# Delta rule recurrence with the decayed state written back into a held PSUM bank, and row scaling in 128-column blocks

## The chip, the cores and the metric

One core of a Trainium2 chip runs the whole kernel. The metric is the device time of one execution in microseconds (us); the median of three runs of the kernel before is 1159.26 us (1158.74 to 1159.27).

## The reference

One transformer-like layer over 1024 tokens of width 1024, in float32. Group A of its mixer is a gated delta rule with 4 heads of 128, evaluated in chunks of 64 tokens; the change lies there. Everything else (modulated RMS norms, the short convolution of group B, the products with `w_out`, a SwiGLU with 2816 hidden channels) is matrix products around it.

```python
def step(state, inp):
    qd, wi, ui, ai, kd, gl = inp
    v_new = ui - jnp.einsum('bhcd,bhde->bhce', wi, state)
    out = jnp.einsum('bhcd,bhde->bhce', qd, state) + jnp.einsum('bhcm,bhme->bhce', ai, v_new)
    state = state * jnp.exp(gl)[..., None, None] + jnp.einsum('bhcd,bhce->bhde', kd, v_new)
    return state, out
...
h = rms_norm(x, norm1_w[l]) * (1.0 + scale1) + shift1
x = x + gate1 * hybrid_mixer(h, ...)
h = rms_norm(x, norm2_w[l]) * (1.0 + scale2) + shift2
x = x + gate2 * swiglu(h, w_gate[l], w_up[l], w_down[l])
return rms_norm(x, norm_f_w)
```

The state of a head is 128 x 128. It is multiplied by the chunk's decay, and the product of the chunk's decayed keys and new values is added to it.

## The kernel before

**Stages.** The tokens are handled in two halves of 512 (`hf` 0 and 1). The first stage, up to about 472 us, is written as tasks (`fill`, `gdn`, `merge`, `output`, `mod_rows`, `gate5` and others). While the program is built, a planner (`Sim`) issues their instructions one by one: it keeps a table of costs, computes for each task when its next operation could start, and takes the earliest; among tasks that could start on that engine at the same time the lower number in `PR` wins. So it decides the order of every engine's instructions, and this order is then fixed. What follows from 472 us on (line 89 for TensorE) is written out by hand in a fixed order, and so is not replanned.

**What TensorE runs in between.** `fill` has the lowest priority and feeds TensorE whenever no other task can: first the products of the normed input with `w_in` (tile `acc`, 128x512 with fp32r operands, three for each 128x128 block), then, when these are used up, the products with `w_out` for tokens 0 to 511 (tile `o`, 8 tiles of 24 products). They take three PSUM banks (0 to 2); all other tasks share five (`chb`).

**The recurrence** (`gdn`) runs once per half, eight chunks in a row (`t` 0 to 3, `cc` 0 and 1), for four heads at once. One step: four products `A` (`WQ` with the state `S`, both read in fp32), VectorE subtracts (`A<-u,A`), ScalarE or VectorE copies the part for the output (`qs`), four products `K` (`kt` with the new values) into a fresh bank, and VectorE updates each head's state by one SCALAR_TENSOR_TENSOR `S<-S,egl,K`. After every second chunk four products `O` follow. Before it, `merge` scales `kt` by row factors into `L`, and later `kt` in place; after it, `output` scales `u` by a row factor, transposes it on TensorE (tile `y`), multiplies it by `zt` and, in the second half, splits it into `at` and `kt` for the products with `w_out`. Each of these three scalings is one VectorE TENSOR_TENSOR over 128x512 with a broadcast factor.

**What hangs on the end of the second recurrence.** When its last `output` is done (`("gdn", 1)`), `mod_rows` builds two rows by ones-products on TensorE (tile `row`), `gate5` loads 16 pieces of `w_ada` of 256 KB through SyncE's queue and accumulates them on VectorE (`A<-Tt,c_act,A` and `aacc<-raw,c_act,aacc`), splits the sums into tiles `Tt`; then SyncE loads `x` for tokens 512 to 1023 (512 KB a tile) and stores the four finished `x` tiles of tokens 0 to 511 to `x_scr` (512 KB each), after which VectorE scales these tiles in place (`x<-x,st,u`). The first buffers of those loads are ones that the `row` products and their splits have read, so the loads wait for them.

**The hand-written part** starts with 24 products `o` (`w_out_tile(4, 1)`), then four `row` products that read `gate5`'s tiles `Tt` (`g5_rows`), 24 more `o` products, and 16 transposes `tr` of the four scaled `x` tiles (`first_half`).

Of the kernel before, what the change touches and what calls it, by code (L numbers as in the profile page):

```python
# [17 lines left out]
P = 128  # L18
# [33 lines left out]
def kernel(  # L52
# [53 lines left out]
    def nm(s):  # L106
        n_id[0] += 1
        return f"{s}_{n_id[0]}"
# [193 lines left out]
    class Sim:  # L302
# [261 lines left out]
    def bank(res, name):  # L564
        return res.tile(psp, [P, HT], F32, name)
# [7 lines left out]
    free = sim.free  # L573

    def ecopy(dst, src):
        sim.either([("act", "copy", nc.scalar.copy, (dst, src), {}), ("dve", "tensor_copy", nc.vector.tensor_copy, (dst, src), {})])
# [6 lines left out]
        ecopy(hi, src)  # L583
        DVE.tensor_tensor(lo, src, hi.bitcast(F32), ALU.subtract)

    def mm(out_, lhsT, rhs, start=True, stop=True):
        PE.matmul(out_, lhsT, rhs, start=start, stop=stop)

    def tr(out_, in_):
        PE.transpose(out_, in_, ident)  # L590
# [583 lines left out]
    def merge(hf, h, T, XA, DD):  # L1174
        st, t_ = sc_[hf], T[h]
        u = us[hf]
        L = t_["L"]
        sim.wait(lambda: ("a", hf, h) in done)
        pP = bank(chb, "P")
        for g in range(2):  # L1180
            mm(v3(pP[:, 32 * g:32 * g + P], 4), L[:, 2 * g + 1, :], bc1(DD[:, 1, 2 * h + g, :], 4))
        ecopy(DD[:, 0, 2 * h:2 * h + 2, :], v3(pP[:, 0:64], 2))
        free(pP)
        Tt = gt("Tt")
        DVE.transpose(flat(Tt), flat(xbd[0][:, 4 * h:4 * h + 4, :]))
        pQ = bank(chb, "Q")
        for g in range(2):
            mm(v3(pQ[:, 32 * g:32 * g + P], 4), XA[:, 2 * h + g, :], bc1(DD[:, 0, 2 * h + g, :], 4))
        for p in range(2):
            for c in range(2):  # L1190
                q = 64 * c + 32 - 32 * p
                ecopy(Tt[64 * c:64 * c + 32, p:4:2, 64 * c + 32:64 * c + 64], v3(pQ[q:q + 32, 0:64], 2))
        free(pQ)
        done.add(("q", hf, h))
        DVE.tensor_tensor(t_["L"], t_["kt"], bc2(t_["bk"], P), ALU.mult)
        free(t_["bk"])
        sim.wait(lambda: ("vt", hf, h) in done)
        pu = bank(chb, "u")
        for t in range(4):
            mm(pu[:, tsl(t)], Tt[:, t, :], u[:, h, t, :])  # L1200
        ecopy(flat(u[:, h]), pu)
        free(pu)
        pw = bank(chb, "w")
        for t in range(4):
            mm(pw[:, tsl(t)], t_["L"][:, t, :], Tt[:, t, :])
        free(t_["L"])
        free(Tt)
        ecopy(t_["WQ"].rearrange("p t (c n) -> p t c n", c=4)[:, :, 0:4:3, :],
                 pw.rearrange("p (t c n) -> p t c n", t=4, c=2))
        free(pw)  # L1210
        DVE.tensor_tensor(t_["kt"], t_["kt"], bc2(st["kd"][:, :, h], P), ALU.mult)
        done.add(("uw", hf, h))

    def gdn(hf):
# [53 lines left out]
        VV = gt("A", (P, 2, 4, P))  # L1268
        V, V1 = VV[:, 0], VV[:, 1]
        POOL.memset(VV, 0.0)  # L1270
        for t in range(4):
            qs = gt("qs")
            if t:
                POOL.memset(V[64:128], 0.0)
            for cc in range(2):
                r0 = 64 * cc
                rv, ro = slice(r0, r0 + 64), slice(64 - r0, 128 - r0)
                W = V1 if cc else V
                first, last = hf == t == cc == 0, hf == cc == 1 and t == 3
                if first:  # L1280
                    ecopy(V[rv], u[rv, :, t, :])
                    POOL.memset(qs[ro], 0.0)
                else:
                    pA = bank(chb, "A")
                    for h in heads:
                        mm(pA[:, tsl(h)], T[h]["WQ"][:, t, cc * P:(cc + 1) * P], S[h])
                    DVE.tensor_tensor(W[rv], u[rv, :, t, :], v3(pA, 4)[rv], ALU.subtract)
                    if cc:
                        ecopy(V[rv], V1[rv])
                    ecopy(qs[ro], v3(pA, 4)[ro])  # L1290
                    free(pA)
                if not last:
                    pK = bank(chb, "K")
                    for h in heads:
                        mm(pK[:, tsl(h)], T[h]["kt"][:, t, :], W[:, h, :])
                    for h in heads:
                        if first:
                            S[h] = gp.tile([P, P], F32, name=nm("S"), tag=f"S{h}", bufs=1)
                            ecopy(S[h], pK[:, tsl(h)])
                        else:  # L1300
                            DVE.scalar_tensor_tensor(S[h], S[h], T[h]["egl"][:, t, cc:cc + 1], pK[:, tsl(h)], ALU.mult, ALU.add)
                    free(pK)
            pO = bank(chb, "O")
            for h in heads:
                mm(pO[:, tsl(h)], T[h]["at"][:, t, :], V[:, h, :])
            DVE.tensor_tensor(u[:, :, t, :], v3(pO, 4), qs, ALU.add)
            free(pO)
            free(qs)
        free(VV)
        for h in heads:  # L1310
            for n in ("at", "WQ", "egl", "kt"):
                free(T[h][n])
# [14 lines left out]
    def output(hf, h, T):  # L1327
        u = us[hf]
        o, nq = u[:, h], T[h]["nq"]
        so, junk, rn = gt("so", (P, 4)), gt("jk", (P, P), BF16), gt("ro", (P, 4))  # L1330
        for t in range(4):
            ACT.activation(junk, o[:, t, :], AF.Square, accum_out=so[:, t:t + 1])
        free(junk)
        DVE.scalar_tensor_tensor(so, so, 1.0 / 128.0, nq, ALU.mult, ALU.add)
        free(nq)
        rsqrt_pow(rn, so, 4)
        DVE.tensor_tensor(o, o, bc2(rn, P), ALU.mult)
        free(so)
# [1057 lines left out]
```

## Time and profile before

| | |
|---|---|
| median of three runs | 1159.26 us |
| span of the profiled execution, first to last instruction | 1158.3 us |
| what lies around the span, against the median | 0.96 us |
| granted TensorE clock, mean | 0.998 |
| first recurrence | about 216 to 258 us |
| second recurrence | about 385 to 429 us |
| planned stage ends, hand-written part begins | 471.7 us |

The profiled execution's own time is not listed beside its span; the difference of 0.96 us is taken as what lies around it. In the profile PE is TensorE's matmul, PEld its weight load, DVE VectorE, ACT ScalarE, POOL GpSimd, SP SyncE and SPq its DMA queue. A row of the chain or the timeline gives start and length in us. An fp32 product appears as two records, so a group of four heads is `x8`. Matmuls are pipelined and overlap in the records, so TensorE's busy share is near 100% wherever they follow each other; how fast it goes is read from the length of a run of equal products.

### The profile page before, as it was taken

The page shows a single profiled execution, that of the slowest core. Times are in us where ns is not written, and L with a number is a line of the kernel's source. Part 1 is how long each engine was busy: PE and PEld are TensorE (multiplying, and loading weights), DVE is VectorE, ACT ScalarE, POOL GpSimd, SP SyncE. Part 2 cuts the span into 40 slices and gives each one's busy share as a digit, 9 for nine tenths or more (in the row PEclk, how much of TensorE's full clock was granted, in tenths as well). Part 3 has the DMA queues.
Part 4 walks back from the last instruction along what each step waited for, and adds up shares of the span by engine and source line. Part 5 has one row for each costly group of instructions (what it writes and reads, how often), then busy time and mean ns, then how long its engine had stood idle before and what let it go on. Part 6 is the DMA issues. An engine that isn't in the chain of part 4 may idle for free.

```text
span 1158.3 us, 16873 instructions
## 1 busy us (share of the span) xinstructions
PE 1148.2 (99%) x5682; PEld 967.1 (83%) x5682; DVE 961.4 (83%) x1820; ACT 565.6 (49%) x1244; POOL 62.3 (5%) x100
## 2 busy tenths in 40 slices
PE   8999999999999999999999999999999999999997
PEld 7888888988888988888888888888888888888886
DVE  7899988999988898669987778877887798688676
ACT  6678732559634543346434443434434455443344
POOL 2110100001101001100000000000000000000002
PEclk9999999999999999999999999999999999999999
DMA  9824456534225546432564457545654599869403
GB/s 363 324 76 143 117 166 174 182 120 138 88 66 164 165 158 210 169 92 72 173 218 163 138 191 231 171 137 175 232 192 143 174 333 394 309 207 337 144 30 146
DMA packets 127544, 209.19 MB, mean 181 GB/s; under 512 B 20577, under 2 KB 45153, under 8 KB 127457
## 3 DMA queue, kind: packets, MB, share of 16 engines
q1 hardware_dynamic: 122080, 204.90, 52.8%
q10 hardware_dynamic: 5376, 3.21, 0.9%
q8 instruction: 45, 0.74, 0.3%
q14 instruction: 43, 0.34, 0.1%
HBM read 153.01 MB, written 55.05 MB: 180 GB/s over the span
## 4 chain that ended last, share of the span: by engine, by line
PE 94%; DVE 3%; ACT 1%; DMA 1%; issue 0%; ACTq 0%; DVEq 0%
PE acc L89 36%; PE acc L448 25%; PE dn L89 17%; PE o L89 4%; PE o L448 3%; PE tr L89 1%; PE K L448 1%; PE A L448 1%; DVE xo L90 1%; PE ab L448 1%; PE w L448 1%; PE u L448 1%; PE kk L448 1%; PE qk L448 1%; DMA raw<-in_w_out_dram 0%; DVE raw L448 0%
## 5 line engine op out<-in xcount | busy, mean ns | idle before, releaser
L448 PE MATMUL acc<-h,u 128*128 128x512 f32 x1200 | 297.9, 397 | 0.0
L448 PEld LDWEIGHTS acc<-h,u 128*128 128x128 f32 x1200 | 220.0, 188 | 42.5 <-issue 0.5
L89 PE MATMUL acc<-h,hl 128*128 128x512 f32 x576 | 135.1, 390 | 0.0
L89 PE MATMUL acc<-T,hl 128*128 128x512 f32 x552 | 130.8, 390 | 0.0
L89 PEld LDWEIGHTS acc<-h,hl 128*128 128x128 f32 x576 | 107.4, 188 | 21.9
L89 PEld LDWEIGHTS acc<-T,hl 128*128 128x128 f32 x552 | 102.4, 188 | 20.4
L90 DVE TENSOR_TENSOR xo<-xo,dn 128x512 f32<-128x512 f32 x84 | 57.0, 684 | 42.3 <-PE dn L89 34.6
L89 PE MATMUL acc<-h,u 128*128 128x512 f32 (+1 forms) x480 | 91.8, 341 | 0.0
L89 PE MATMUL dn<-h,h 128*128 128x512 f32 x396 | 90.7, 389 | 0.0
L89 PEld LDWEIGHTS acc<-h,u 128*128 128x128 f32 x480 | 78.3, 189 | 11.7
L89 PEld LDWEIGHTS dn<-h,h 128*128 128x128 f32 x396 | 74.3, 188 | 15.4
L90 DVE TENSOR_TENSOR cc<-cc,acc 128x512 f32<-128x512 f32 x66 | 41.4, 645 | 32.0 <-PE acc L89 32.0
L448 ACT CAST u<-raw 128x512 fp32r<-128x512 f32 x58 | 35.9, 621 | 56.9 <-PE acc L448 55.1
L448 DVE TENSOR_TENSOR u<-raw,u 128x512 fp32r<-128x512 f32 x82 | 56.1, 685 | 4.0 <-ACT u L448 3.5
L89 PE MATMUL acc<-T,u 128*128 128x512 f32 x240 | 56.0, 389 | 0.0
L448 DVE SCALAR_TENSOR_TENSOR cv<-pr,cols_a,cv 128x512 f32<-128x512 f32 x72 | 53.8, 756 | 0.3
L89 PEld LDWEIGHTS acc<-T,u 128*128 128x128 f32 x240 | 45.1, 188 | 9.3
L90 ACT CAST h<-rw 128x512 fp32r<-128x512 f32 x57 | 32.7, 618 | 41.3 <-PE dn L89 34.6
L90 ACT CAST hl<-S 128x512 fp32r<-128x512 f32 x44 | 25.3, 623 | 56.2 <-DVE S L90 56.2
L90 ACT ACTIVATE cc<-cc 128x512 f32<-128x512 f32 x33 | 20.9, 633 | 64.0 <-DVE cc L90 64.0
L90 ACT CAST u<-R 128x512 fp32r<-128x512 f32 (+1 forms) x60 | 34.2, 585 | 35.3 <-DVE R L90 34.2
L90 DVE TENSOR_TENSOR hl<-S,hl 128x512 fp32r<-128x512 f32 x44 | 28.5, 687 | 26.3 <-ACT hl L90 26.3
(377 smaller groups left out, 2145.1 us busy)
## 6 DMA issues: line engine op xcount, KB each, us to landing
raw<-in_w_in_dram SPq DMA_DIRECT2D x82, 256.0 KB, 3.3
am_scr<-cc SPq DMA_DIRECT2D x77, 256.0 KB, 4.3
raw<-in_w_ada_dram SPq DMA_DIRECT2D x56, 256.0 KB, 3.1
rw<-am_scr SPq DMA_DIRECT2D x55, 256.0 KB, 5.0
rw<-bm_scr SPq DMA_DIRECT2D x53, 256.0 KB, 5.1
bm_scr<-raw SPq DMA_DIRECT2D x51, 256.0 KB, 5.5
R<-in_w_gate_dram SPq DMA_DIRECT2D x22, 512.0 KB, 4.3
R<-in_w_up_dram SPq DMA_DIRECT2D x22, 512.0 KB, 5.5
```

The costliest lines, as they stand in the source:

```text
L89: return call(*a, **k)
L90: ins = call(*a, **k)
L448: ins = call(*a, **k)
```

## The change

A new helper `erows` scales a 128x512 tile by row factors in four blocks of 128 columns. Each block goes to ScalarE (ACTIVATE Copy with a column as scale) or to VectorE (TENSOR_SCALAR), as the planner finds earlier. It takes the place of the three TENSOR_TENSORs in `merge` and `output`.

In `gdn` one PSUM bank `K` is held for the whole recurrence of a half. The first `K` products open it; all later ones add onto what stands there. After each step the whole bank is copied into one state tile `S` (128x4x128; by ScalarE or VectorE, whichever is earlier), and ScalarE writes each head's state, scaled by the next chunk's decay, back into the bank, in four ACTIVATEs. The SCALAR_TENSOR_TENSOR stays only in the first step of the second half, where the state comes from the first half. The last step of a half, or the one before it, needs no write-back.

```diff
+    def erows(dst, src, cols):
+        for t in range(4):
+            escale(dst[:, t, :], src[:, t, :], cols[:, t:t + 1])
...
-        DVE.tensor_tensor(t_["L"], t_["kt"], bc2(t_["bk"], P), ALU.mult)
+        erows(t_["L"], t_["kt"], t_["bk"])
...
-        DVE.tensor_tensor(t_["kt"], t_["kt"], bc2(st["kd"][:, :, h], P), ALU.mult)
+        erows(t_["kt"], t_["kt"], st["kd"][:, :, h])
...
+        pK = bank(chb, "K")
         for t in range(4):
...
-                        mm(pA[:, tsl(h)], T[h]["WQ"][:, t, cc * P:(cc + 1) * P], S[h])
+                        mm(pA[:, tsl(h)], T[h]["WQ"][:, t, cc * P:(cc + 1) * P], S["t"][:, h, :])
...
                 if not last:
-                    pK = bank(chb, "K")
+                    opens = t == cc == 0
                     for h in heads:
-                        mm(pK[:, tsl(h)], T[h]["kt"][:, t, :], W[:, h, :])
-                    for h in heads:
-                        if first:
-                            S[h] = gp.tile([P, P], F32, name=nm("S"), tag=f"S{h}", bufs=1)
-                            ecopy(S[h], pK[:, tsl(h)])
-                        else:
-                            DVE.scalar_tensor_tensor(S[h], S[h], T[h]["egl"][:, t, cc:cc + 1], pK[:, tsl(h)], ALU.mult, ALU.add)
-                    free(pK)
+                        mm(pK[:, tsl(h)], T[h]["kt"][:, t, :], W[:, h, :], opens and h == 0, True, not opens or h > 0)
+                    if first:
+                        S["t"] = gp.tile([P, 4, P], F32, name=nm("S"), tag="S", bufs=1)
+                    if opens and not first:
+                        for h in heads:
+                            DVE.scalar_tensor_tensor(S["t"][:, h, :], S["t"][:, h, :], T[h]["egl"][:, t, cc:cc + 1], pK[:, tsl(h)], ALU.mult, ALU.add)
+                    else:
+                        ecopy(flat(S["t"]), pK)
+                    t2, c2 = (t, 1) if cc == 0 else (t + 1, 0)
+                    if not (hf == 1 and t2 == 3 and c2 == 1) and t2 < 4:
+                        for h in heads:
+                            ACT.activation(pK[:, tsl(h)], S["t"][:, h, :], AF.Copy, scale=T[h]["egl"][:, t2, c2:c2 + 1])
...
-        DVE.tensor_tensor(o, o, bc2(rn, P), ALU.mult)
+        erows(o, o, rn)
```

TensorE's products are the same in number and kind, and so are GpSimd's and SyncE's instructions. Their order changes, because the planner sees other costs. Two places on TensorE matter below.

The first is one step of the second recurrence, from the last `K` product of the third step to the `A` products of the next. Before:

```order
L448 MATMUL K_4334<-A_4211,kt_3439 128x128
L448 MATMUL acc_4308<-h_1_140_761,u_4090 128x512 x2
L448 MATMUL acc_4308<-h_1_145_787,u_4231 128x512 x3
L448 MATMUL acc_4308<-h_1_147_793,u_4231 128x512 x2
L448 MATMUL A_4368<-S_2416,WQ_2848 128x128
L448 MATMUL A_4368<-S_2420,WQ_2849 128x128
```

The same place on TensorE in the changed kernel:

```order
L448 MATMUL K_4320<-A_4314,kt_3497 128x128
L448 MATMUL acc_4482<-h_1_131_720,u_4363 128x512
L448 MATMUL acc_4482<-h_1_138_754,u_4363 128x512 x3
L448 MATMUL acc_4482<-h_1_140_761,u_4363 128x512 x3
L448 MATMUL acc_4482<-h_1_145_787,u_4401 128x512 x3
L448 MATMUL A_4521<-S_2451,WQ_2972 128x128
```

Seven filling products stood between `K` and `A`, and now ten do. From a recurrence's first product to its last `O` stood 110 filling products in the first half and 117 in the second; now 148 and 150 do.

The second place is on TensorE from the first `row` product of `mod_rows` to its last. Before:

```order
L448 MATMUL row_4850<-raw_4834,ones 128x512
L448 MATMUL o_4842<-h_1_839_4527,h_0_744_4024 128x512
L448 MATMUL o_4842<-h_1_845_4556,h_0_754_4064 128x512 x3
L448 MATMUL o_4842<-h_1_850_4584,h_0_758_4079 128x512
L448 MATMUL row_4850<-raw_4835,ones 128x512
L448 MATMUL o_4842<-h_1_850_4584,h_0_758_4079 128x512 x2
L448 MATMUL o_4842<-h_1_855_4630,h_0_773_4155 128x512 x2
L448 MATMUL row_4867<-raw_4863,ones 128x512
L448 MATMUL o_4842<-h_1_855_4630,h_0_773_4155 128x512
L448 MATMUL o_4842<-h_1_866_4663,h_0_776_4168 128x512
L448 MATMUL row_4867<-raw_4864,ones 128x512
```

After this last `row` product 80 products `o` follow before the hand-written part begins, that is the rest of tile `o_4842` and three whole tiles. The same place on TensorE now:

```order
L448 MATMUL row_4977<-raw_4966,ones 128x512
L448 MATMUL o_4953<-h_1_834_4636,h_0_757_4155 128x512
L448 MATMUL o_4953<-h_1_836_4652,h_0_769_4217 128x512
L448 MATMUL row_4977<-raw_4967,ones 128x512
L448 MATMUL o_4953<-h_1_836_4652,h_0_769_4217 128x512 x2
L448 MATMUL o_4953<-h_1_838_4678,h_0_774_4247 128x512 x2
L448 MATMUL row_4994<-raw_4990,ones 128x512
L448 MATMUL o_4953<-h_1_838_4678,h_0_774_4247 128x512
L448 MATMUL o_4999<-h_1_816_4508,h_0_729_4024 128x512
L448 MATMUL row_4994<-raw_4991,ones 128x512
```

Behind it only 23 products `o` are left, all of the last tile `o_4999`, before the hand-written part begins. From the first `row` product to that point stand 95 products before (4 `row`, 91 `o`), and 35 now (4 `row`, 31 `o`). From the last `O` product to the first transposes `y` stood 27 products `o`, and now 22. SyncE's order of the loads and stores named above is the same before and after.

More of the change, by code (lines that the diff above doesn't have):

```diff
@@ L584, in esplit, with mm @@
         DVE.tensor_tensor(lo, src, hi.bitcast(F32), ALU.subtract)
-    def mm(out_, lhsT, rhs, start=True, stop=True):
-        PE.matmul(out_, lhsT, rhs, start=start, stop=stop)
+    def mm(out_, lhsT, rhs, start=True, stop=True, more=False):
+        PE.matmul(out_, lhsT, rhs, start=start, stop=stop, skip_group_check=more)
+    def erows(dst, src, cols):
+        for t in range(4):
+            escale(dst[:, t, :], src[:, t, :], cols[:, t:t + 1])
     def tr(out_, in_):
@@ L1309, in gdn @@
         free(VV)
+        free(pK)
         for h in heads:
```

## Prediction

> **What bounds the kernel now.** The first part of the page says that TensorE is busy all the time, and VectorE nearly so.
>
> ```profile
> PE 1148.2 (99%) x5682; PEld 967.1 (83%) x5682; DVE 961.4 (83%) x1820; ACT 565.6 (49%) x1244; POOL 62.3 (5%) x100
> ```
>
> A mean says nothing on the two recurrences, so I read the busy time by stretches: the first recurrence, the second, and a long stretch of plain products (columns: stretch, its length, PE, PEld, DVE, ACT, POOL, clock, DMA share, GB/s).
>
> ```profile
> 200.00:262.00 62.00, 62.00 (x399) 55.36 (x398) 59.25 (x118) 32.99 (x79) 3.03 (x5) 1.00 0.49 154
> 394.00:436.00 42.00, 41.80 (x246) 36.07 (x245) 39.41 (x80) 19.91 (x49) 3.95 (x5) 1.00 0.49 162
> 545.00:942.00 397.00, 397.00 (x1930) 336.07 (x1928) 329.11 (x529) 168.08 (x322) 0.00 (x0) 1.00 0.54 181
> ```
>
> VectorE is at 96% and 94% in the recurrences, ScalarE at about half. Is TensorE held by VectorE there? I need the length of an undisturbed product. The chain that ended last, in order of time, gives it, and the end of the planned stage with it.
>
> ```profile
> 388.20 0.89 PE K L448 x8
> ...
> 444.62 0.44 PE y L448 x4
> 445.06 5.04 PE o L448 x22
> 450.10 0.23 PE row L448
> ...
> 453.57 18.14 PE o L448 x80
> 471.71 5.59 PE o L89 x24
> 477.31 0.94 PE row L89 x4
> 478.24 5.57 PE o L89 x24
> 483.82 1.75 PE tr L89 x16
> ```
>
> A 128x512 product takes 18.14/80 = 0.227 us, a group `K`, `A` or `O` of four heads 0.89 us, four transposes 0.44 us. Now the groups of TensorE in the second recurrence, from 394 to 436 us:
>
> ```profile
> L448 PE MATMUL acc<-h,u 128*128 128x512 f32 x75 | 20.7, 407 | 0.0
> L448 PE MATMUL o<-wu,h 128*128 128x512 f32 x31 | 9.3, 399 | 0.0
> L448 PE MATMUL A<-S,WQ 128*128 128x128 f32 x48 | 6.6, 277 | 0.0
> L448 PE MATMUL o<-L,h 128*128 128x512 f32 x16 | 5.4, 395 | 0.0
> L448 PE MATMUL K<-A,kt 128*128 128x128 f32 x40 | 5.3, 276 | 0.0
> L448 PE MATMUL O<-A,at 128*128 128x128 f32 x32 | 4.2, 274 | 0.0
> ```
>
> 122 x 0.227 + 15 x 0.89 + 0.44 for the first `y` is 41.5 us of work in 42.0. So the recurrence costs TensorE no more than its products: the filling products cover every wait. The kernel is bound by TensorE's work, which the change leaves as it is. It can only gain the gaps, some 0.5 us here and, taken alike, about 1 us in the two recurrences together, or lose by a new gap.
>
> **The change part by part.** *VectorE and ScalarE in the recurrence.* The groups with the prices:
>
> ```profile
> L448 DVE SCALAR_TENSOR_TENSOR S<-S,egl,K 128x128 f32<-128x128 f32 x56 | 15.6, 340 | 1.2 <-PE K L448 1.1
> L448 DVE TENSOR_TENSOR kt<-kt,kd 128x512 f32<-128x512 f32 x8 | 5.5, 682 | 0.0
> ```
> ```profile
> L448 ACT ACTIVATE u<-vT,bv 128x128 f32<-128x128 f32 x22 | 6.8, 367 | 2.3 <-PE vT L448 1.5 <-DVE u L448 0.8
> L448 ACT COPY u<-u 128x512 f32<-128x512 f32 x8 | 4.7, 582 | 0.1
> ```
>
> 52 of the 56 state updates go, 52/56 x 15.6 = 14.5 us of VectorE. 14 copies of a whole bank (in place of four 128-column ones) and 52 write-backs come to ScalarE. No row shows ScalarE writing PSUM; the nearest, a scaled 128-column block out of PSUM, takes 367 ns, and 0 is the floor. I take 0.37: 52 x 0.37 + 14 x 0.58 = 27 us over some 100 us, of which ScalarE has half free. The write-back must precede the next `K`, the copy the next `A`. Between stand, in the new order, ten products (2.3 us) from `K` to `A` against 0.6 us for the copy, and about 5 us from `K` to `K` against 0.6 + 4 x 0.37 = 2.1 us. Cover enough: cost 0. If ScalarE came late, the four `A` and all filling products behind them would wait, since TensorE's queue is in order.
>
> *Row scaling.* 24 TENSOR_TENSORs of 0.68 us become 96 blocks (by the order 62 on VectorE, 34 on ScalarE). They precede products with filling work around them: 0. The exception is `output` of the second half, below.
>
> *The order.* This is the part that I expect to cost. The planner puts 38 and 33 more filling products into the two recurrences. Filling products are not made, they are taken from behind: after the second recurrence only 35 products stand from the first `row` product to the hand-written part, where 95 stood. What has to happen meanwhile on the other engines does not shrink. The timeline of it in the kernel before (start, length, engine):
>
> ```profile
> 450.32 0.33 SPq L448 DMA_DIRECT2D raw<-in_w_ada_dram  x1
> ```
> ```profile
> 467.32 0.69 DVE L448 TENSOR_TENSOR Tt<-aacc,Tt 128x512 fp32r<-128x512 f32 x1
> 473.02 1.28 DVE L448 SCALAR_TENSOR_TENSOR x<-x,st,u 128x1024 f32<-128x1024 f32 x1 [4.41 <-DMA x_scr<-x]
> 478.56 1.28 DVE L448 SCALAR_TENSOR_TENSOR x<-x,st,u 128x1024 f32<-128x1024 f32 x1 [1.27 <-DMA x_scr<-x]
> ```
>
> The gated loads of `w_ada` start with the first `row` product (450.10), since their buffers are read by it and by the splits behind it. `gate5`'s tiles are ready at 468.01, that is 17.9 us after it. TensorE wanted them 27.2 us after it (477.31): 9.3 us to spare. The first scaled `x` starts at 22.9 us, when its store to `x_scr` has landed; the last ends at 479.84, 4 us ahead of the transposes at 483.82.
>
> In the changed kernel TensorE gets from the first `row` product to its first `row` product of the hand-written part in 35 x 0.227 + 5.6 = 13.5 us, and to the transposes in 13.5 + 0.94 + 5.57 = 20.0 us. The 17.9 us stand against the 13.5: a wait of 4.4 us. For the scaled `x` I need the DMA's rate.
>
> ```profile
> 430.00:435.00 5.00, 5.00 (x23) 3.89 (x21) 3.98 (x9) 3.17 (x18) 1.39 (x2) 1.00 0.98 376
> ...
> 460.00:465.00 5.00, 5.00 (x24) 4.14 (x23) 5.00 (x9) 0.00 (x0) 0.00 (x0) 1.00 0.96 338
> 465.00:470.00 5.00, 5.00 (x24) 4.14 (x23) 3.57 (x6) 3.95 (x7) 1.02 (x3) 1.00 0.98 347
> ```
> ```profile
> x<-in_x_dram SPq DMA_DIRECT2D x8, 512.0 KB, 6.9
> raw<-in_w_ada_dram SPq DMA_DIRECT2D x8, 256.0 KB, 5.1
> x_scr<-x SPq DMA_DIRECT2D x4, 512.0 KB, 8.4
> ```
>
> The DMA engines are full, at 340 GB/s. Behind the 16 pieces of `w_ada` (4.2 MB) SyncE's queue holds four `x` loads (2.1 MB) and the four stores (2.1 MB). A store takes 0.524 MB / 340 GB/s = 1.54 us. In the kernel before, the fourth waited for the last `o` tile; now all adds are done by then, so they land one after the other: the fourth tile is scaled by 22.9 + 3 x 1.54 + 1.28 = 28.8 us. TensorE comes at 20.0, and 0.3 us of transposes of the first three tiles can go ahead: 28.8 - 20.0 - 0.3 = 8.5 us in all, the 4.4 among them. Bounds: at 376 GB/s throughout, 8.4 MB take 22.3 us, and the tile is scaled at 0.2 + 22.3 + 1.3 = 23.8, a loss of 3.8 us; at the mean from 450.32 to 473.02 (6.55 MB, 289 GB/s) also for the stores, 9.3 us.
>
> [...]
>
> *The `y` transposes.* They follow the last `O` after 22 products (5.0 us) instead of 27 (6.1 us). The rows:
>
> ```profile
> 427.91 1.05 PE L448 MATMUL O<-A,at 128*128 128x128 f32 x8
> 435.29 0.63 PE L448 MATMUL y<-ident,u 128*128 128x128 f32 x4 [0.20 <-DVE u L448]
> ```
> Before, 27 products from 428.7 end at 434.8 and `y` starts at 435.3, 6.6 us behind `O`: 0.5 us lost. In that time lie the add, four squares, the root on GpSimd and the scaling, and VectorE's queue held two of them up. Now VectorE's queue is lighter, but ScalarE's has three casts of `WQ` between the squares. Ends: 5.0 us, no wait, and 6.6 us as before, 1.6 lost. I take 5.9, 0.9 lost, 0.4 more than before.
>
> **Sum.** 8.5 + 0.4, less 0.4 us of gaps that the freed VectorE closes (0 to 1), and 0.2 us because VectorE's additions queue behind the late scalings: 8.7 us. On the span 1158.3 + 8.7 = 1167.0; with the 0.96 us around it, which is how the profiled execution stands to the median, 1168.0 us.
>
> **The rivals.** *Not slower: freeing VectorE pays more.* Place: the two stretches of 62 and 42 us. If VectorE paced the products there, closing the weight load's idle 6.6 + 5.9 = 12.5 us would outweigh the tail: 1168.0 - 12.5 = 1155.5. It decides as soon as 8.7 of these 12.5 us are real. For it: VectorE's 96% and 94%. Against it: 545 to 942 us has the same weight-load share (336 of 397, 85%) with no recurrence at all, and the sum above leaves 0.5 us of 42. [...] With all smaller versions, down to no change: 0.10.
>
> *Only the smaller wait.* The loads or stores go faster, so that little beyond the `row` wait is left: 3.8 to 4.4 us, about 1163.5. For it: 376 GB/s have been reached once, and the mean of 289 to the first store shows that the queue was not full from the start. Against: the two later stretches are at 340 with the same transfers. 0.12.
>
> *ScalarE becomes the recurrence's limit.* Its queue is in order: a cast that waits for a `w_out` load holds up the copy of the state, and 14 steps at 0.5 us add 7 us: 1175. For it: in the kernel before the update sits in VectorE's queue, which stands behind the same loads. Against: ScalarE is half idle, and TensorE stays about 2 us behind each copy. 0.10.
>
> *The forecast*, both waits in the tail: 0.68.
>
> **Range and chances.** Its low end is the smaller-wait case, 3.8 us of tail less a full 1 us of closed gaps and some of the 0.2 and 0.4: 1159.26 + 3.2 = 1162.5. Its high end is 9.3 us of tail, 1.1 more at `y`, and 2.8 us, 0.2 for each of 14 steps, if ScalarE's copies are a little late: 1159.26 + 13.2 = 1172.5; left out are the rival of no loss and the ScalarE case. A difference of 0.2%, 2.3 us, is about what a measurement of this kernel can tell from no change. Slower by more: 0.68 + 0.12 + 0.10 = 0.90; the other 0.10 I split into 0.05 within 0.2% and 0.05 faster.
>
> **What would show it.** Right: the chain names a `row` product (line 89) that waits for VectorE's `Tt` by 4 to 5 us, and the first `tr` that waits for the last scaled `x`, another 4; from the first `row` product of `mod_rows` to the `Tt` again about 18 us; VectorE in the second recurrence well below 94%; the stretch 545 to 942 shifted as a whole, with the same length. Wrong: no wait at these two places, or the planned stage itself longer than 471.7 us by more than 2 us, which would be ScalarE in the recurrence; or the second recurrence at fewer us per product than 0.227.

## The result, and the profile after

The changed kernel takes 1172.47 us (median of four runs, 1171.17 to 1174.72) against 1159.26 us before: 1.0114 times as long, with a 95% interval of 1.0100 to 1.0129, or 13.2 us slower. The forecast was 1168.0, so the direction and the main place were right, while the loss is half as large again as the 8.7 us of the sum. The profiled execution took 1173.0 us; its span is 1171.2 us, 12.9 more than before. (So 1.8 us lie around a span. The 0.96 us named ahead of the prediction is a difference between one execution's span and the median of others; the 8.7 us do not hang on it.)

The first part of the page: VectorE has lost 5 us of work in all, ScalarE has gained 28, and TensorE's products are the same in number.

```profile
PE 1151.4 (98%) x5682; PEld 966.9 (83%) x5682; DVE 956.3 (82%) x1820; ACT 593.6 (51%) x1326; POOL 57.8 (5%) x100
```

The stretches that answer to those of before (length, PE, PEld, DVE, ACT, POOL, clock, DMA share, GB/s): the first recurrence, 42 us of the second, and the plain products.

```profile
200.00:262.00 62.00, 61.27 (x382) 53.93 (x381) 57.24 (x111) 43.51 (x102) 3.03 (x5) 1.00 0.53 171
...
394.00:436.00 42.00, 39.82 (x228) 33.54 (x228) 33.40 (x57) 25.79 (x54) 1.43 (x3) 1.00 0.60 196
...
551.00:951.00 400.00, 400.00 (x1950) 338.81 (x1949) 332.22 (x533) 170.21 (x326) 0.00 (x0) 1.00 0.53 177
```

VectorE falls from 39.4 to 33.4 us in these 42 us, as foreseen, but TensorE does less there, not more: 39.8 of 42 us, where it was 41.8. The second recurrence lasted from 384.6 to 428.7 us before, so that the last 7 us of the prediction's stretch lay behind it; now it lasts from 390.8 to 445.5. Taken over its whole length, VectorE goes from 94% to 72%. The plain products are busy throughout, as before.

Where the 12.9 us went can be counted on TensorE alone. For each product I take the time to the start of the next one, less the median of that time for products of its shape in the kernel before, and add this up by stage. This "lost" time contains idle time and slow products alike. Both profiles hold the same products, so the sums can be compared (us lost):

| stage on TensorE | before | after | change |
|---|---|---|---|
| start to the first `K` | 8.0 | 7.4 | -0.5 |
| first recurrence | 0.5 | 1.1 | +0.6 |
| between the recurrences | 0.6 | 0.7 | +0.1 |
| second recurrence | 0.7 | 3.8 | +3.0 |
| last `O` to the first `row` | 0.5 | 0.2 | -0.3 |
| first `row` to the `row` that reads `Tt` | 0.2 | 3.5 | +3.3 |
| from there to the first `tr` of `x` | 0.2 | 1.9 | +1.7 |
| 30 us from that `tr` on | 0.4 | 1.9 | +1.4 |
| 30 to 65 us from it | 0.4 | 3.7 | +3.3 |
| the rest | -0.3 | -0.3 | 0 |
| sum | 11.2 | 23.8 | +12.7 |

The tail (the four lines of the table from the first `row` on) has lost 9.8 us, the recurrences 3.6. First the tail. The chain that ended last runs from the first `row` product through the loads of `w_ada` and the stores of `x` to the scaling of `x`:

```profile
466.57 0.25 PE row L448
...
467.73 4.70 DMA raw<-in_w_ada_dram
...
473.99 5.75 DMA Tt<-in_w_ada_dram
479.76 8.33 DMA x_scr<-x
...
488.21 1.17 DVE x L448
```

And TensorE's timeline of the same place, with its idle time and who ended it in brackets:

```profile
479.78 0.39 PE L89 MATMUL o<-wu,kt 128*128 128x512 f32 x1
483.29 2.37 PE L89 MATMUL row<-Tt,ones 128*128 128x512 f32 x4 [3.12 <-ACT Tt L448]
485.46 3.42 PE L89 MATMUL o<-h,WQ 128*128 128x512 f32 x12
...
491.50 0.84 PE L89 MATMUL tr<-ident,x 128*128 128x128 f32 x3
493.22 1.64 PE L89 MATMUL tr<-ident,x 128*128 128x128 f32 x13 [0.89 <-DVE x L448]
```

Both waits of the forecast are there: 3.3 us at the `row` product, 3.1 of them idle (forecast 4.4), and 1.4 at the transposes (forecast 4.1). Something is between them that the sum did not have. Four `row` products take 2.2 us to the next start, not 0.9, and the `o` products behind are slow as well. The stretches around the wait show the granted clock:

```profile
479.80:483.00 3.20, 0.37 (x2) 0.00 (x0) 3.15 (x5) 1.00 (x2) 0.00 (x0) 1.00 0.94 362
...
484.00:485.00 1.00, 1.00 (x3) 0.83 (x3) 0.00 (x0) 1.00 (x3) 0.54 (x2) 0.50 0.98 401
485.00:486.00 1.00, 1.00 (x4) 0.77 (x3) 0.00 (x0) 1.00 (x3) 0.47 (x2) 0.50 1.05 430
...
487.00:488.00 1.00, 1.00 (x6) 0.80 (x5) 0.00 (x0) 0.41 (x2) 0.92 (x3) 1.00 1.01 414
```

Behind 3.1 idle us TensorE's clock is at half: the trace has it at 0.50 from 483.05 to 486.47 us, that is for 3.4 us. The last column matters too: the DMA engines move 401 to 430 GB/s here.

The third loss of the tail lies 45 us further on, in the hand-written part. In the kernel before, 16 transposes of `raw` tiles ran without a gap (first fence); now TensorE waits three times (second):

```profile
528.64 1.91 PE L89 MATMUL tr<-ident,raw 128*128 128x128 f32 x16
```
```profile
537.96 0.49 PE L89 MATMUL tr<-ident,raw 128*128 128x128 f32 x3
539.52 1.64 PE L89 MATMUL tr<-ident,raw 128*128 128x128 f32 x13 [1.07 <-DVE raw L90]
...
544.82 1.15 PE L89 MATMUL tr<-ident,x 128*128 128x128 f32 x8 [0.89 <-ACT raw L90]
546.71 1.22 PE L89 MATMUL tr<-ident,x 128*128 128x128 f32 x8 [0.75 <-DVE raw L90]
```

VectorE is late there, and I followed its queue back. At the transposes of `x` it is about 3 us behind TensorE: its addition of the second `o` tile starts 3.4 us after the first `tr` (494.87 against 491.50), where it was 0.2 us (483.85 against 483.65), since the four scalings stand ahead of it. The addition after, and then before:

```profile
494.87 0.68 DVE L90 TENSOR_TENSOR x<-x,o 128x512 f32<-128x512 f32 x1
```
```profile
483.85 0.69 DVE L90 TENSOR_TENSOR x<-x,o 128x512 f32<-128x512 f32 x1 [2.21 <-PE o L89]
```

It is still behind, though by less, when a 256 KB half of `x` that it has finished is stored through ScalarE's queue; VectorE scales that tile in place after the store has landed. That store among the DMA issues (the last column is the time to landing), after, and then before:

```profile
x_scr<-x ACTq DMA_DIRECT2D x1, 256.0 KB, 4.5
```
```profile
x_scr<-x ACTq DMA_DIRECT2D x1, 256.0 KB, 2.0
```

The same store takes 4.5 us instead of 2.0. Before, it went out at 511.15, ahead of the weight load `R` at 512.13; now it goes out at 521.86, behind `R` at 521.45. `R` waits for TensorE, the store for VectorE. Of VectorE's 3 us some 1.4 are left at this place (the store goes out 0.4 us behind `R` instead of 1.0 ahead), and that is enough for the two to change places. Why the store takes 2.5 us longer behind `R` is not shown.

Then the recurrences. The largest gap, in ScalarE's timeline (first fence) and TensorE's (second):

```profile
426.20 0.62 ACT L448 CAST h<-raw 128x512 fp32r<-128x512 f32 x1 [2.98 <-DVE raw L448]
426.84 0.59 ACT L448 COPY S<-K 128x512 f32<-128x512 f32 x1
427.46 1.58 ACT L448 ACTIVATE K<-S,egl 128x128 f32<-128x128 f32 x4
```
```profile
426.18 0.40 PE L448 MATMUL o<-L,h 128*128 128x512 f32 x1
427.48 1.16 PE L448 MATMUL A<-S,WQ 128*128 128x128 f32 x8 [0.90 <-ACT S L448]
```

The state's copy could have run from about 424 us, when `K` ended, but ahead of it in ScalarE's order is a cast that waited 2.98 us for VectorE, which waited for a load of `w_out` (issued at 418.66, landed after 6.73 us). Three `K` products of the second recurrence, and one of the first, wait 0.5 to 0.6 us for VectorE's subtraction; in the second recurrence it stands, in the same way, behind work on late loads. How much this costs differs from one execution to another: four of the kernels below have the changed kernel's order on TensorE, VectorE and ScalarE up to 445 us, and three of them (stores first, stores first with earlier loads, extra products) lose 2.5 us in the second recurrence instead of 3.8.

### The profile page after: what moved, and what is told of

The parts are those of the page before. It is cut to its first block, busy times and chain, and to the rows that moved or that the text cites. A ratio compares the mean times of both kernels' runs of the same rounds, so it can differ in the third digit from the quotient of the medians.

```text
span 1171.2 us, 16952 instructions
## 1 busy us (share of the span) xinstructions
PE 1151.4 (98%) x5682; PEld 966.9 (83%) x5682; DVE 956.3 (82%) x1820; ACT 593.6 (51%) x1326; POOL 57.8 (5%) x100
## 4 chain that ended last, share of the span: by engine, by line
PE 81%; DVE 8%; DMA 6%; ACT 2%; issue 2%; SPq 0%; ACTq 0%; POOL 0%; DVEq 0%; POOLq 0%
PE acc L89 35%; PE acc L448 22%; PE dn L89 17%; PE o L448 2%; DMA x_scr<-x 2%; DMA raw<-in_w_out_dram 1%; DMA raw<-in_w_ada_dram 1%; DVE x L90 1%; DMA wa<-in_w_mod_dram 1%; DVE xo L90 1%; PE ab L448 1%; PE kk L448 1%; PE qk L448 1%; DVE raw L448 1%; PE K L448 1%
## 5 line engine op out<-in xcount | busy, mean ns | idle before, releaser
L89 PEld LDWEIGHTS acc<-h,u 128*128 128x128 f32 x480 | 78.3, 189 | 11.7
```

The lines of the kernel that those rows point to most:

```text
L89: return call(*a, **k)
```

## The experiments

Two kernels do one part of the change each. Each ratio is to executions of the kernel before that were taken along with the experiment (medians of 1159.5 to 1160.0 us), so experiments are best compared by their ratios, and the changed kernel's is 1.0114.

**The row scaling alone** (the kernel before with `erows`).

```diff
-        DVE.tensor_tensor(t_["L"], t_["kt"], bc2(t_["bk"], P), ALU.mult)
+        erows(t_["L"], t_["kt"], t_["bk"])
...
-        DVE.tensor_tensor(o, o, bc2(rn, P), ALU.mult)
+        erows(o, o, rn)
```

> The kernel before with the row scaling in blocks alone, and the old recurrence. First theory (the loss comes from filling products that are moved from behind the second recurrence into it, so that the gated loads of w_ada and the stores of x come too late): the planner puts 105 and 108 filling products into the two recurrences here, as before (106 and 106), and 87 (before 91) stand between the first row product and the hand-written part, so nothing is lost: 1159.3 us, 1158 to 1161. Rival (ScalarE's and VectorE's 96 small blocks cost by themselves): 2 us or more slower, 1161.5 to 1164.

Measured: 1162.96 us, ratio 1.0027 (1.0016 to 1.0037), 3.2 us slower. The rival was right. The tail has no wait, as the first theory had it; the loss lies ahead of the second recurrence's first `K`, where TensorE loses 11.7 us instead of 9.1. What it waits for between 200 and 400 us, where the kernel before has no such wait (us in total, times, longest us):

```profile
PE K L448 <- DVE A L448: 0.6, 1, 0.6
PE ada L448 <- DVE raw L448: 0.5, 1, 0.5
PE A L448 <- DVE S L448: 0.5, 1, 0.5
PE y L448 <- ACT u L448: 0.3, 1, 0.3
```

Why the blocks do not relieve VectorE is seen in the groups of the changed kernel:

```profile
L448 DVE TENSOR_SCALAR L<-kt,bk 128x128 f32<-128x128 f32 x20 | 5.0, 316 | 0.1
L448 DVE TENSOR_SCALAR u<-u,ro 128x128 f32<-128x128 f32 x21 | 5.0, 282 | 0.5 <-POOL ro L448 0.5
L448 DVE TENSOR_SCALAR kt<-kt,kd 128x128 f32<-128x128 f32 x21 | 4.7, 280 | 0.0
L448 ACT ACTIVATE L<-kt,bk 128x128 f32<-128x128 f32 x12 | 4.4, 397 | 0.2
L448 ACT ACTIVATE kt<-kt,kd 128x128 f32<-128x128 f32 x11 | 3.9, 405 | 0.0
L448 ACT ACTIVATE u<-u,ro 128x128 f32<-128x128 f32 x11 | 3.8, 392 | 1.0 <-POOL ro L448 1.0
```

Four blocks on VectorE take 4 x 0.28 = 1.1 us, one whole operation took 0.68. So 62 of 96 blocks still cost VectorE 14.7 us, where 24 operations cost 24 x 0.68 = 16.4, and ScalarE pays 12.1 us on top. (With the row scaling alone it is 58 blocks and 13.5 us on VectorE.) That the blocks cost 3.2 us by themselves is shown; the four waits hold 1.9 us of it, and which block holds up which of them was not tried. In the changed kernel this loss does not return: up to the same `K` TensorE loses 9.2 us there, about as much as before.

**The held bank alone** (the changed kernel with the old row scaling).

> The changed kernel with the old row scaling: the held bank alone. 137 and 141 filling products in the recurrences (changed kernel 144 and 139), 55 between the first row product and the hand-written part (changed 31, before 91). First theory: TensorE reaches its first row product of the hand-written part 55 x 0.227 + 5.6 = 18 us after the first row product, no wait there (in the changed kernel Tt is ready after 16.9 us); the transposes of x at 24.6 us, the last scaled x at 26.6, so some 1.7 us there and 2 to 3 us later from VectorE's late additions, and the 3.6 us of gaps of the two recurrences: 1167 us, 1164 to 1169. Rival (the recurrence itself carries the loss, the tail only swallows it): as slow as the changed kernel, 1171 to 1174.

Measured: 1164.73 us, ratio 1.0043 (1.0029 to 1.0056), 5.0 us slower. The first theory holds for the tail, but the 3.6 us of gaps that it counted in the recurrences are not there: they lose 0.6 and 0.5 us (before 0.5 and 0.7), so the write-backs cost nothing there. There is no wait at the `row` product, 0.4 us at the transposes, and 3.1 us more than before at 513 to 548 us: the late VectorE again.

Four kernels move the loads and stores of the tail.

**`gate5` not waiting for `row`**, in the changed kernel and in the kernel before.

```diff
-        sim.wait(lambda: len(us0) == KB and len(us1) == KB and "row" in done)
+        sim.wait(lambda: len(us0) == KB and len(us1) == KB)
```

> The changed kernel with gate5 no longer waiting for the row products, so that its loads are issued earlier; TensorE's order is the same, 31 products between the first row product and the hand-written part. First theory: the wait of the row product (3.3 us), the slow products behind it (1.7), the wait of the transposes of x (1.4) and most of the 3.3 us later, from VectorE's late additions, go; the recurrences' 3.6 us stay: 1172.5 - 9 = 1163.5 us, 1162 to 1166. Rival (the tail only waits for work that is late anyway, since ScalarE paces the recurrence): 1170 to 1173.

> The kernel before with the same edit of gate5. First theory: its loads were in time before (9.3 us to spare at the row product, 4 us at the transposes), so earlier loads gain nothing: 1159.3 us, 1158 to 1160.5. Rival (earlier loads are worth something by themselves, for instance because the end of the stage is crowded with transfers): 1157 or less.

Measured: 1177.22 us, ratio to the kernel before 1.0149 (1.0135 to 1.0163), and 1159.90 us, 1.0002 (0.9994 to 1.0011). The second is as expected: the kernel before had time to spare. The first is a miss, 14 us off. The `row` product's wait is gone (0.2 us lost), but half of the loads now go out inside the recurrence, ahead of what it needs. From the changed kernel's waits:

```profile
DVE aacc L448 <- DMA raw<-in_w_ada_dram: 4.1, 2, 3.8
...
PE K L448 <- DVE A L448: 3.8, 1, 3.8
```

VectorE stands at the first accumulation until its load has landed, the subtraction of the recurrence stands behind it, and `K` waits 3.8 us; in the four us from 443 on the clock is at 0.65, 0.50, 0.50 and 0.64. The scaled `x` come no earlier either, since their stores still follow everything else (5.5 us more loss than before in the 30 us from the first `tr`). So the theory was too simple: what stands behind each wait matters, and which transfer is last in the queue.

**The stores of `x` ahead of the loads of `x`** in SyncE's queue; no other instruction moves. In the changed kernel, and with the held bank alone.

```diff
         dma(x2_scr[t], x2[t])
+        done.add(("st", t))
...
-            sim.wait(lambda: ... (t < 4 or ("g5", 0) in done and ("g5", 1) in done))
+            sim.wait(lambda: ... (t < 4 or all(("st", i) in done for i in range(4))))
```

> The changed kernel; the four stores of x to x_scr now stand ahead of the four loads of x in SyncE's queue, and nothing else moves on any engine. Theory (in the tail the scaled x tiles set the end, and they wait for their stores, which stand last in the queue; VectorE's additions behind them are late by 3.1 us, and so is all up to 550 us): the stores go out at 476.5 us instead of 479.8, the scaling starts at about 485.5 instead of 488.2, the wait of the transposes (1.4 us) and most of the 3.3 us behind go: 1168 us, 1167 to 1169.5; the wait of the row product (3.3) and the slow products behind it (1.7) stay. Rival (not the stores but the row product's wait is what costs, the rest follows from it): 1171 to 1173.

> The held bank alone (old row scaling), with the same exchange in SyncE's queue. Its trace shows no wait at the row product and 0.4 us at the transposes, but 3.1 us some 45 us later, at transposes of raw tiles that VectorE delivers late. Theory (VectorE is late there because the four scalings of x waited for their stores; its own next store then collides with a weight load and lands 2 us later): the scalings come about 2.5 us earlier, and the 3.5 us go: 1164.7 - 3.5 = 1161.2 us, 1160 to 1162.5. Rival (the loss some 45 us later has its own cause): 1164 to 1165.5.

Measured: 1171.19 us, 1.0101 (1.0085 to 1.0116), and 1161.52 us, 1.0019 (1.0010 to 1.0028). The second is as expected: 3.2 us less than the held bank alone (the late loss falls from 3.1 to 2.1 us there, and the wait at the transposes goes; the rest of the 3.2 us is spread over stages that this edit does not touch). So a part of that late loss comes from the scalings that waited for stores. The first is a miss, in the rival's range. The transposes wait no longer, the scaling starts at 483.47 us instead of 488.21, but the 3.3 us further on stay (the weight load goes out at 518.60, the store at 518.86), so the median falls by 1.3 us only and its interval overlaps that of the changed kernel. What the theory left out: the four scalings now wait for their statistics on ScalarE and GpSimd, which come behind the split of `Tt`; VectorE is still 1.6 us behind (491.75 against a first `tr` at 490.12), enough for the weight load to pass the store.

**Both: stores first, and `gate5` waiting for the last `output`** instead of `row`.

> The changed kernel with the same exchange, and with gate5 waiting for the end of the last output instead of the row products, so that its loads may be issued some us earlier, but not inside the recurrence. Theory: the row product's wait and the slow products behind it go as well (5 us), the transposes wait 0 to 1 us, VectorE is late by up to 2 us: 1165 us, 1162.5 to 1167; left are the gaps of the recurrences (3.6 us). Rival (earlier loads only move the wait to another place, as when they were put into the recurrence): 1168 or more.

Measured: 1168.02 us, 1.0075 (1.0062 to 1.0088). Gone are the `row` product's wait (0.3 us lost) and most of the slow products (0.9); 1.6 us at the transposes and 3.7 us further on remain. TensorE is earlier, and the rest of the chain only partly follows: the time is 1 us above the theory's range, at the rival's edge.

**Extra products in the wait**: 14 products that TensorE runs ahead of `row`, for nothing but to be busy.

```diff
     keep_x2(4, (1,))
+    hot = bank_tile(6, "heat")
+    for _ in range(14):
+        pmm(hot, ones_r, us1[KORD[0]][0], True, True)
     g5_rows()
```

> The changed kernel with 14 extra products (14 x 0.227 = 3.2 us, their result is not used) ahead of the row product that waits 3.3 us. Theory (the granted clock of 0.5 for 2.5 us behind the wait comes from the wait itself, but the scaled x tiles, not TensorE, set the time of the transposes): the row and o products behind go at 0.227 us with the clock at 1.0, TensorE reaches the transposes 1.7 us earlier and waits that much longer there: no change, 1171.5 to 1173.5. Rival (the slow products are on the path): 1169.5 to 1171.

Measured: 1172.09 us, 1.0105 (1.0091 to 1.0118): no change, as the theory said. The interval reaches into the rival's range (up to 1171), so the trace has to decide. TensorE's timeline and the clock:

```profile
479.24 3.42 PE L89 MATMUL heat<-L,ones 128*128 128x512 f32 x14
482.81 1.17 PE L89 MATMUL row<-Tt,ones 128*128 128x512 f32 x4
483.82 2.94 PE L89 MATMUL o<-h,WQ 128*128 128x512 f32 x12
...
490.72 0.33 PE L89 MATMUL tr<-ident,x 128*128 128x128 f32 x1 [0.90 <-DVE x L448]
...
493.20 1.64 PE L89 MATMUL tr<-ident,x 128*128 128x128 f32 x13 [0.92 <-DVE x L448]
```
```profile
484.00:485.00 1.00, 1.00 (x6) 0.79 (x6) 0.00 (x0) 1.00 (x3) 0.22 (x1) 1.00 0.98 397
```

With TensorE busy the clock stays at 1.0 (482 to 487 us), and the 12 `o` products behind take 2.94 us instead of 3.42. TensorE waits for three scaled tiles at the transposes instead of one; the thirteen last ones start 27.6 us after the first `row` product (493.20 - 465.63), in the changed kernel 26.8 us (493.22 - 466.41). So the slow clock comes from the wait, and the scaled `x`, not TensorE, set this place.

**The one store through SyncE's queue**, right ahead of the weight load, in the changed kernel and in the held bank with stores first.

```diff
-            ACT.dma_start(out=x2_scr[t][:, cs], in_=x2[t][:, cs])
+            (SP if t == 6 and ch == 0 else ACT).dma_start(out=x2_scr[t][:, cs], in_=x2[t][:, cs])
```

> The changed kernel with one 256 KB store to x_scr (tile 6, first half) issued through SyncE's queue, where it stands right ahead of the first weight load R, instead of ScalarE's. Theory (in the changed kernel that load goes out 0.4 us ahead of the store, the store lands in 4.4 us instead of 2, VectorE scales in place 2 us later, and the transposes of raw tiles some 12 us further on wait 3.3 us in all): the load can't pass the store any more, 2 of the 3.3 us go: 1170.2 us, 1169 to 1171.3. Rival (VectorE is late there by the four scalings alone, 3.1 us, whatever the store does): no change, 1171.5 to 1173.5.

> The held bank alone, stores of x ahead of the loads of x, and the same store through SyncE's queue. Theory: the 2 us that were left in that kernel (its store went out in the same 0.1 us as the weight load and landed after 3.9 us) go, and with them the whole loss of the held bank: 1159.5 us, 1158.5 to 1160.5, the time of the kernel before. Rival (the held bank costs something in the recurrence too): 1161 or more.

Measured: 1170.36 us, 1.0088 (1.0074 to 1.0102), and 1160.96 us, 1.0010 (1.0001 to 1.0019). The store goes out at 522.27 ahead of the load at 522.70 (511.65 and 512.09 in the other), and the tile is scaled 2.9 and 3.0 us after the issue, where it was 4.65 (521.86 to 526.51). In the changed kernel the first wait is gone:

```profile
538.43 1.91 PE L89 MATMUL tr<-ident,raw 128*128 128x128 f32 x16
...
543.49 1.15 PE L89 MATMUL tr<-ident,x 128*128 128x128 f32 x8 [0.41 <-ACT raw L90]
545.38 1.22 PE L89 MATMUL tr<-ident,x 128*128 128x128 f32 x8 [0.74 <-DVE raw L90]
```

The loss at 30 to 65 us falls from 3.7 to 1.9 us. So the change of places cost about 2 us of the 3.3. With the held bank the time falls by 0.6 us (by 1.0 by the ratios, whose intervals overlap) instead of 2, to just above the theory's range; 1.5 us more than before are still lost at the two later waits. Their cause, beyond a VectorE that is still late, I have not tested.

**The recurrence**: the planner told that each load of `w_out` lands 3 us later.

```diff
         dma(r, wout[k * P:(k + 1) * P, cs])
+        for use in sim.acc[r.tensor.name]:
+            use[4] += 3.0 if use[5] else 0.0
```

> The changed kernel, with the planner told that each load of w_out lands 3 us later than it thinks; the recurrences hold 144 and 136 filling products, 30 stand behind the first row product, so the tail is as in the changed kernel. Theory (the 3 us of new gaps in the second recurrence are K and A products that wait for VectorE or ScalarE, whose queues are in order and stand at an operation on a w_out load that lands after 5 to 7 us): these operations are placed behind the recurrence's own, and 2.5 to 3 us of gaps go: 1169.6 us, 1168.5 to 1171. Rival (the write-backs on ScalarE or the copy of the state are what is late, whatever the loads do): 1171.5 to 1174.

Measured: 1169.92 us, 1.0087 (1.0074 to 1.0101), as the theory said. The second recurrence, with the same write-backs and copies on ScalarE, has no gap left: 47.0 of 47.0 us, where the changed kernel had 48.8 of 51.0 (first fence the experiment, second the changed kernel).

```profile
394.00:441.00 47.00, 47.00 (x277) 41.21 (x277) 36.01 (x60) 29.21 (x64) 1.56 (x3) 1.00 0.53 175
```
```profile
394.00:445.00 51.00, 48.82 (x280) 41.41 (x280) 36.43 (x61) 28.80 (x63) 1.56 (x3) 1.00 0.50 161
```

TensorE loses 0.5 us in it, as it does with all four edits; the six kernels with both parts and the planner's old landing times lose 2.5 to 8.6. The tail is as in the changed kernel.

**All four edits together.**

> The changed kernel with four edits together: loads of gate5 from the end of the last output on, stores of x ahead of the loads of x, the one store through SyncE's queue, and the planner told that w_out loads land 3 us later. Theory (the losses lie at separate places and add up): from the kernel with the first two edits (1168.0 us), 2 us at the store and 2 us of gaps in the second recurrence go: 1164.0 us, 1162.5 to 1165.5; what then stands against the kernel before is mostly what the row scaling alone cost (3.2 us). Rival (a gain at one place is lost again at the next, since all meet at the transposes): 1166.5 or more.

Measured: 1166.83 us, 1.0058 (1.0045 to 1.0072): 1.2 us less than with the first two edits (2.0 by the ratios) instead of 4. The time is in the rival's range, and the trace shows the rival's mechanism. The last piece of `w_ada` is in use 14.6 us after the first `row` product (464.60 to 479.17) instead of 12.9 (465.13 to 478.01), so the wait that the second edit had removed is back, and behind it the clock is at 0.66, 0.50, 0.50 and 0.64 in the four us from 482 on. Counted from the same `row` product, it goes out 0.5 us later, and it lands after 7.6 instead of 6.4 us; why was not tested.

```profile
478.35 0.49 PE L89 MATMUL row<-Tt,ones 128*128 128x512 f32 x1 [0.22 <-ACT Tt L448]
480.58 1.27 PE L89 MATMUL row<-Tt,ones 128*128 128x512 f32 x3 [1.73 <-DVE Tt L448]
```

No version of the change beats the kernel before; the nearest is the held bank with two of the edits, 0.1% behind. This fits the bound: TensorE's products fill the time, and before the change only some 3 us were lost after the first 216 us.

## Why the prediction was right and where it was not

**TensorE is the bound, a freed VectorE gains nothing:** right. VectorE is at 80% instead of 94% in the stretch of the second recurrence, and nothing was gained. Of the 12.5 us of idle weight load that the first rival had at stake none came, and by the table only 1.2 us were lost in the two recurrences before. The 0.4 us of gaps that the sum took off were not gained there either.

**Filling products are taken from behind, so the tail comes early for its loads:** right as a mechanism. The `row` product wants `Tt` 13.4 us after the first `row` product (forecast 13.5; 466.57 to 480.0) and its tiles are finished after 17.4 us (17.9; VectorE's last split ends at 483.96). It waits 3.3 us and not 4.4, since the first of the four products needs only the first tile, which ScalarE casts. The held bank alone, with 55 products at this place instead of 31, does not wait.

**"28.8 - 20.0 - 0.3 = 8.5 us in all":** the term of the scaled `x` was sized too high. The last one is ready after 26.6 us, not 28.8. The first scaling starts after 21.6 us instead of 22.9 (488.21), and the stores land 1.2 us apart instead of 1.54. I took the DMA at 340 GB/s, and at 376 for the low bound, the highest of the stretches that I had read. Others are higher: the kernel before moves 402 GB/s from 432 to 437 us and 425 from 470 to 473, and its first three stores, too, land 1.24 us apart (472.90, 474.14, 475.38). The changed kernel moves 401 to 430 here. (The low bound of 3.8 us also leaves out the 0.3 us that the 8.5 takes off.) Up to the transposes the tail loses 3.3 + 1.7 + 1.4 = 6.4 us, of which 1.7 is the slow clock. That term was missing in the sum, though it did not lengthen it: with the extra products, at a clock of 1.0, TensorE idles 2.7 us at the transposes (0.90 + 0.91 + 0.92) instead of 0.9.

**"and 0.2 us because VectorE's additions queue behind the late scalings":** this step failed. It is 3.3 us. I counted the queue's delay at its place and took it for absorbed. VectorE carries a part of its 3 us along, and 27 us later (494.87 to 521.86) the 1.4 us that are left make a store and a load change places, which adds 2 us and brings the delay to TensorE's transposes. The one store through the other queue shows these 2 us; the exchange of stores, with the held bank alone, shows that the late scalings have a part in the delay. The cause of the rest, 1.5 us or more at the two later waits, stays open.

**"Cover enough: cost 0" in the recurrence:** failed, by 3.6 us, though the prices were right. The write-back takes 371 ns (0.37) and the copy 583 ns (0.58), together 27.5 us (27):

```profile
L448 ACT ACTIVATE K<-S,egl 128x128 f32<-128x128 f32 x52 | 19.3, 371 | 1.9 <-DVE S L448 0.4
L448 ACT COPY S<-K 128x512 f32<-128x512 f32 x14 | 8.2, 583 | 7.1 <-PE K L448 7.0
```

The cover was counted against these lengths, not against what stands ahead in the queue. This is the third rival in a weaker form: it had 0.5 us at each of 14 steps; there were four gaps of 0.5 to 1.1 us in the second recurrence, one at the copy and three at VectorE's subtraction. The held bank alone has none of them, and the later landing times remove them with both parts in place. So it is the order that the planner found, with loads that land later than it reckons, and not the work on ScalarE.

**"They precede products with filling work around them: 0" for the row scaling:** failed. Alone it costs 3.2 us. I priced the removed operations and not the blocks, four of which are dearer on VectorE than one whole operation. Put on top of the held bank it costs 7.7 us (1164.73 to 1172.47; 8.9 between the two profiled spans), but at other places: by TensorE's lost time 3.2 more in the second recurrence and 6 in the tail up to 30 us from the first `tr`, less some 0.7 at the start.

**The `y` transposes, +0.4:** wrong in sign, and small. Between the last `O` and the first `row` 0.2 us are lost, 0.3 less than before.

**The signs that were named.** The two waits came, smaller than named (3.3 for 4 to 5, 1.4 for 4); `Tt` came after 17.4 us (18); VectorE went well below 94%; the plain products were shifted as a whole. But one sign of being wrong came too: the planned stage ends 2.9 us later than before (the first product of line 89 starts at 474.42 instead of 471.55), more than the 2 us that were set. It was to mean ScalarE in the recurrence. Of the four gaps there one is at ScalarE's copy, the others are at VectorE, and both engines stand behind late loads.

So 1168.0 came from a right mechanism with one term too large (8.5 for 6.4) and two taken at about nothing: 3.6 us in the recurrences and 3.3 in the hand-written part. That 1172.47 still lies in the range, whose end is 1172.5, is luck: that end was added up from 9.3 us of tail, 1.1 at `y` and 2.8 of late copies, and measured were 6.4, -0.3 and 3.6, with the 3.3 us of the hand-written part, for which the range held nothing. The parts do not add up: 3.2 alone and 5.0 alone make 13.2 together. Only together do they leave so few products behind the first `row` product (31, against 91 before, 87 with the row scaling alone and 55 with the held bank alone), and only together does the second recurrence have its gaps.

## What to carry to other kernels

Where the bound engine is full, filling its gaps in one place takes cover away from another; list what must happen behind the place that loses its products, and compare in us. Price a wait not only at its length: ask whose queue is delayed, how far down that delay is carried, and which two transfers will change places. Where an engine's order is fixed, as here, the question is not how long the new operation takes but what stands ahead of it and what that is waiting for.

## What the runs showed of the hardware

In the changed kernel TensorE's granted clock was 0.50 from 483.05 to 486.47 us, that is for 3.4 us, behind a wait of 3.3 us (waits here are counted from start to start, as in the table); products of 128x512 started 0.43 us apart in it instead of 0.227. With `gate5` not waiting for `row` (3.8 us of idle time ahead) and with all edits together (a wait of 2.0 us; another 0.4 us of waiting and one product stand just ahead of it) the stretches of 1 us given above add up to 3.4 us at 0.50 each time. With the stores first, behind a wait of 2.7 us, the clock was 0.50 from 484 to 485 us, and with the one store through SyncE's queue from 485.8 to 486.8. It stayed at 1.0 behind waits of 1.1 us in the changed kernel (products at 427.48 and 539.52 us), and from 487 to 491 us with stores first and earlier loads, where TensorE stood idle for all of the first us. With `gate5` not waiting the mean clock of the whole execution was 0.994, in the changed kernel 0.998.

A scaling by a column on VectorE took 0.28 us for 128x128 (`kt` and `u`; `L` 0.32), so that four blocks cost 1.1 us where one product with a broadcast factor over 128x512 took 0.68. ScalarE wrote a scaled 128x128 block into PSUM in 371 ns in the changed kernel; reading one from there took 367 ns in the kernel before.
